# The first 512 up columns begun on two tiles of 128 tokens, the third tile following, with the next columns and the conv weights moved forward

## The chip, the cores and the metric

The kernel runs on one core of one Trainium2 chip. What counts is the device time of one execution, in microseconds (us), read as the median of several runs. The engines are PE (TensorE: matmuls, and transposes as matmuls with an identity), DVE (VectorE), ACT (ScalarE), POOL (GpSimd) and SP (SyncE, which issues almost all weight loads as DMAs). Each engine works off its own instructions in a fixed order; an instruction that has to wait holds up everything behind it on the same engine. SBUF is the on-chip memory that the engines read, PSUM the small memory (8 banks) that PE writes its products to.

## The reference

One layer of a flow-matching trunk on 384 tokens (128 context tokens, 256 latent tokens) with 2048 channels, in float32:

```python
def _layer(x, mod, grid, s_ret0, c0, n0, m0, lp):
    ...
    sh1, sc1, g1, sh2, sc2, g2 = jnp.split(mod, 6, axis=-1)
    h = _ln(x) * (1.0 + sc1) + sh1
    mix, states = _mixer(h, ...)                       # w_in, heads, out = (...) @ w_out
    x = _ln(ALPHA * x + g1 * mix) * ln1_g + ln1_b
    h = _ln(x) * (1.0 + sc2) + sh2
    x = _ln(ALPHA * x + g2 * _ffn(h, ...)) * ln2_g + ln2_b

def _ffn(h, grid, w_up, conv_ff, w_down):
    ug = h @ w_up                                      # 2048 x 2*5504
    u, g = ug[..., :D_FF], ug[..., D_FF:]
    return (jax.nn.silu(_seq_conv(u, conv_ff, grid)) * g) @ w_down
```

The vectors `sh1 ... g2` come from `mod = silu(c) @ w_mod + b_mod`, one set for the context tokens and one for the latent ones. The convolution has 3 taps along the tokens.

## The kernel before, in words

**Precision.** Each float32 operand is split in a high part (`hi`, `ah`: a cast, on ACT) and a rest (`lo`, `al`: source minus high part, on DVE or POOL; the helper's line is L118), and each product is three matmuls: high by high, and the two mixed ones.

**Tiles.** The 384 tokens are three tiles of 128. In the projections up and in, a weight block 128x128 is PE's stationary operand and all 384 tokens move past it, so the product comes out transposed, with channels on the partitions (`psu`, L182 to L184, 128x384). The projections out (`w_out`) and down keep a tile of tokens stationary and move 512 weight columns (L190 to L192).

**Weights.** One load is 512 KB, 128x1024 elements (for the up projection 4 blocks of 128 rows by 256 columns, a "group" here). It goes into one of 4 `raw` buffers, is cast into one of 3 `hi` buffers and subtracted into one of 3 `lo` buffers. SP issues the loads in order; a load waits until its `raw` buffer is free.

**Around the change.** The last 512 columns of `w_out` are done tile by tile with all weights already split (five groups in buffers of their own, `wxh` and `wxl`, three in `hi` and `lo`). After each tile comes its norm chain, `norms(tt)`: DVE scales the product by the gate, adds it to the residual `r` and takes statistics; POOL raises the variance to the power -1/2 (`brs`, L200), DVE applies the first norm in two passes over 128x2048 (L981, L983), takes statistics again (`xst`, L1063), adds epsilon (`veps`, L198), POOL's power comes again, DVE makes the scaled mean `nm` (L963) and ACT writes the normalised tile in four pieces (L1069: into `g1b` for tile 0, `xn` for tile 1, `l1g` for tile 2). `h2_piece` then takes 128 channels of a tile: PE transposes them into a bank of the 3-bank pool `pat` (`xtp`, L114), ACT (or DVE) applies scale and shift (`h`, 5 buffers), ACT casts `ah`, POOL (or DVE) makes `al`.

The first 512 up columns (256 of u, 256 of g) need all three tiles, since all 384 tokens move in one matmul; the pieces of tiles 1 and 2 are made together then (128x256, on DVE). Their products lie in the 5-bank pool `pmm`. `up_gate` applies convolution, silu and gate to u and g (DVE: L345, L349, L1159, and the split of the result, `fal`). The other up columns follow, 256 of u and 256 of g at a time; "the second 512 columns" below are the next ones.

**The vector sums.** Besides, the vector g2 of `mod` (`mods5`) is summed on DVE: 32 loads `mraw` of 512 KB by SP (3 buffers), and for each two passes of 128x1024 (`macc`: L283 for the first load, L286 after). They are not needed before the final residual, but stand in DVE's and SP's order from the first up columns on.

**Order.** The program states dependences and a written order; a scheduler that estimates times fixes the order on each engine when the program is built. `issue_after` holds an instruction's place in that order behind another's. So the order is not that of the source, and a changed source moves instructions elsewhere too.

**The names the change touches.** `norms` and `h2_piece` (above), `ps_first` (the banks of the first 512 columns), `up_product` and `up_gate`, `mod_from_rows` (scale and shift vectors read back from memory: `mfr`, then a transpose `mfp`), and `cfr`, `pcf`, `cfw` (conv weights: load, transposes, copy).

Of the kernel before, what the change touches and what calls it, by code (L numbers as in the profile page):

```python
# [21 lines left out]
NT = T // P  # L22
# [60 lines left out]
def hybrid_step(ctx, tc, ca, cb, x_prompt, x_sample, state_ret, state_c, state_n, state_m, c, c_ctx,  # L83
# [3 lines left out]
    nc = tc.nc  # L87
# [5 lines left out]
    wraw = pool("wraw", 4)  # L93
# [12 lines left out]
    ident = cst[:, C_ID:C_ID + P]  # L106
# [4 lines left out]
        return prompt[0] if tt == 0 else sample[0, (tt - 1) * P:tt * P, :]  # L111

    def transpose(out, in_, n=P):
        nc.tensor.transpose(out, in_, ident[:n, :n])  # L114

    def split(dst_hi, dst_lo, src, eng=None):
        nc.scalar.copy(dst_hi, src)  # L117
# [17 lines left out]
    def rows_bcast(dst, src_row, n):  # L135
        nc.gpsimd.dma_start(out=dst, in_=src_row.to_broadcast([P, n]))
# [34 lines left out]
    act_hi = [None] * KT  # L171
    act_lo = [None] * KT
# [6 lines left out]
    def mm_a(ps, w, kk, width, m, ah, al, start, stop):  # L179
        hi, lo = w  # L180
        s = slice(kk * width + m * P, kk * width + (m + 1) * P)
        nc.tensor.matmul(ps, lhsT=hi[:, s], rhs=ah, start=start, stop=False)  # L182
        nc.tensor.matmul(ps, lhsT=hi[:, s], rhs=al, start=False, stop=False)  # L183
        nc.tensor.matmul(ps, lhsT=lo[:, s], rhs=ah, start=False, stop=stop)  # L184

    def mm_b(ps, w, kk, ah, al, tt, start, stop, c0=0, n=512):
        hi, lo = w
        s = slice(kk * 512 + c0, kk * 512 + c0 + n)
        t = slice(tt * P, (tt + 1) * P)
        nc.tensor.matmul(ps, lhsT=ah[:, t], rhs=hi[:, s], start=start, stop=False)  # L190
        nc.tensor.matmul(ps, lhsT=ah[:, t], rhs=lo[:, s], start=False, stop=False)  # L191
        nc.tensor.matmul(ps, lhsT=al[:, t], rhs=hi[:, s], start=False, stop=stop)  # L192
# [2 lines left out]

    def rstd(out, var, n=1):
        v = small.tile([P, NT], F32, tag="veps", name="veps")
        nc.vector.tensor_scalar(out=v[:, :n], in0=var, scalar1=EPS, scalar2=None, op0=ALU.add)  # L198
        with tc.high_priority():
            mark["pow"] = nc.gpsimd.tensor_tensor(out=out, in0=v[:, :n], in1=mhalf[:, :n], op=ALU.pow).ins  # L200

# [119 lines left out]
            yield from g  # L321

    def mod_from_rows(part, n, psp, sbp, name, plus):
        rows = sbp.tile([2 * KT, P], F32, tag="mfr", name="mfr", bufs=1)
        for v in range(2):
            nc.sync.dma_start(out=rows[v * n:(v + 1) * n, :], in_=modrow[part, v, :n * P].rearrange("(k p) -> k p", p=P))
        ps = psp.tile([P, 2, n], F32, tag="ps", name="mfp")
        transpose(ps.rearrange("p v k -> p (v k)"), rows[:2 * n, :], 2 * n)
        nc.vector.tensor_scalar(out=modf[name][:, :, :n], in0=ps, scalar1=plus, scalar2=None, op0=ALU.add)
# [613 lines left out]

    rp = pool("rp", 1, reuse_waits="tile")
    r = [rp.tile([P, D], F32, name=f"r{tt}") for tt in range(NT)]

    rstat = [rp.tile([P, 5, 6], F32, name=f"rst{tt}") for tt in range(NT)]

# [37 lines left out]
    with ExitStack() as p2:  # L986
# [23 lines left out]
        def w_out_block(nb):  # L1010
            ps = pso if nb == 0 else [(pat if nb == 1 else pmm).tile([P, 512], F32, tag="ps", name="pso")
                                      for _ in range(NT)]
            for k0 in (12,) if nb == 0 else range(0, KT, 2):
                part_b(ps, weights_b(wo, k0, 2, (nb * 512,)), 2, k0, 0, KT - 1 if nb else 13)
                if nb > 0:
                    mods4.step()
                if k0 == (10 if nb else 12):
                    residual_loads(nb)
                if nb == 2 and k0 == 14:
                    residual_loads(3)  # L1020
                if nb == 1 and k0 == 8:
# [17 lines left out]
        for i in range(KT // 2):  # L1039
            raw = wraw.tile([P, 1024], F32, tag="raw", name="raw")  # L1040
            nc.sync.dma_start(out=raw.rearrange("p (k n) -> p k n", k=2),
                              in_=wo[2 * i * P:(2 * i + 2) * P, 1536:2048].rearrange("(k p) n -> p k n", p=P))
            if i < KT // 2 - 3:
                hi = wx.tile([P, 1024], F32R, name=f"wxh{i}")
                lo = wx.tile([P, 1024], F32R, name=f"wxl{i}")
                split(hi, lo, raw)
                ws.append((hi, lo))
            else:
                ws.append(split_weights(raw))
        xn = [None] * NT  # L1050

        def norms(tt):
            residual(sb2, g1b, tt, 3, ps[tt], True, True)
            if tt == NT - 1:
                mark["pb1"] = mark["pow"]
            st = post_stats(tt)
            if tt == NT - 1:
                mark["pa2"] = mark["pow"]
            for s in post_norm(tt, st, l1g, l1b, 1):
                pass  # L1060
            xst = small.tile([P, 4, 6], F32, tag="bst", name="xst")
            for j in range(4):
                nc.vector.bn_stats(out=xst[:, j, :], in_=r[tt][:, j * 512:(j + 1) * 512])  # L1063
            mv, rs = aggr(xst)
            nm = neg_scaled_mean(mv, rs)
            t = l1g if tt == NT - 1 else g1b[:, 0, :] if tt == 0 else xnp.tile([P, D], F32, tag="xn", name="xn")
            for j in range(4):
                s = slice(j * 512, (j + 1) * 512)
                nc.scalar.activation(t[:, s], r[tt][:, s], AF.Identity, bias=nm, scale=rs)  # L1069
            xn[tt] = t  # L1070
# [20 lines left out]

        for tt in range(NT):
            for kt in range(KT):
                mm_b(ps[tt], ws[kt // 2], kt % 2, act_hi[kt], act_lo[kt], tt, kt == 0, kt == KT - 1)
                if tt == NT - 1 and kt >= 5:
                    h2_piece(0, kt - 5)
            norms(tt)
        for kt in range(KT - 5, KT):
            h2_piece(0, kt)
        for kt in range(5):  # L1100
            h2_piece(1, kt)
        wu, wd = w_up[0], w_down[0]
        ps_first = [pmm.tile([P, T], F32, tag="ps", name="psu") for _ in range(2)]
        wg = None
        for i in range(KT + 2):
            if i < 5:
                h2_piece(2, i)
            elif i < KT:
                h2_piece(1, i, 2)
            if i == KT - 1:  # L1110
                mark["h2"] = mark["lo"]
            kt = i - 2
            if kt < 0:
                continue
            if kt % 4 == 0:
                if kt < 12:
                    with tc.issue_after(mark["pb1"] if kt < 4 else mark["pa2"]):
                        wg = weights_a(wu, kt, 4, 0, 256)
                else:
                    wg = weights_a(wu, kt, 4, 0, 256)  # L1120
            for m in range(2):
                mm_a(ps_first[m], wg, kt % 4, 256, m, new_hi[kt], new_lo[kt], kt == 0, kt == KT - 1)
        act_hi[:], act_lo[:] = new_hi, new_lo


# [3 lines left out]
    ffp = pool("ffp", 12, p3, reuse_waits="tile")  # L1129
    sb3 = pool("sb3", 2, p3, reuse_waits="tile")  # L1130
    acc = [g2p.tile([P, D], F32, name=f"acc{tt}") for tt in range(NT)]
    cfr = sb3.tile([NF, 3, P], F32, tag="y", name="cfr")
    nc.gpsimd.dma_start(out=cfr, in_=conv_ff[0].rearrange("t (f p) -> f t p", p=P))
    cfw = g2p.tile([P, 3, NF], F32, name="cfw")
    pcf = pat.tile([P, 3, NF], F32, tag="ps", name="pcf")
    for t in range(3):
        transpose(pcf[:, t, :], cfr[:, t, :], NF)
    nc.vector.tensor_copy(cfw, pcf)
    def up_product(pool_, ug, f0, n):
        cols = n * P  # L1140
        ps = [pool_.tile([P, T], F32, tag="ps", name="psu") for _ in range(n)]
# [21 lines left out]
            out.append((ah, al))  # L1163
        return out

    a = up_gate(0, ps_first, up_product(pmm, 1, 0, 2))
    psum_a.close()
    pps = pool("pps", 8, p3, space=PSUM, reuse_waits="tile")

    def ups(f0, n):  # L1170
        out = []
        for f in range(f0, f0 + n, 2):
            m = min(2, f0 + n - f)
            us = up_product(pps, 0, f, m)
            out += up_gate(f, us, up_product(pps, 1, f, m))
        return out

# [43 lines left out]
    ws = []  # L1221
# [64 lines left out]
```

## Time and profile before

| what | value |
|---|---|
| median of 3 runs | 2062.88 us (2061.55 to 2065.3) |
| profiled execution | 2066.21 us, of it span 2064.4 us |
| mean granted TensorE clock | 0.982 |
| PE busy | 1988.4 us (96%) |
| DVE busy | 1231.4 us (60%) |
| ACT busy | 694.1 us (34%) |
| POOL busy | 233.0 us (11%) |
| last matmuls of w_out begin | 921.44 us |
| first up matmul | 941.33 us |
| first 512 up columns end | 979.07 us |
| second 512 up columns end | 1017.3 us |

Positions in the table are microseconds from the start of the profiled span. In rows of a timeline the first number is the start, the second the length, then engine, line, operation, out<-in, shape and count; square brackets give the idle time before it and what ended it. In the view of stretches each engine has its busy time and its count; the last three columns are the granted TensorE clock (1.00 is full), the DMA engines' busy share and GB/s. Matmuls overlap, so the time that one costs is the distance between starts, not its length.

### The profile page before, as it was taken

To read this page: it belongs to the slowest core of one execution; us is meant where nothing else is said; L and a number is where in the kernel's file an instruction comes from. 1 tells how busy PE (TensorE), PEld (TensorE's weight loads), DVE (VectorE), ACT (ScalarE), POOL (GpSimd) and SP (SyncE) were. 2 spreads that over 40 slices of the span, in tenths; PEclk is the share of its full clock that TensorE was granted. 3 is DMA by queue.
4 is the path that set the end of the run, shared out by engine and by line. 5 is a ranking of instruction groups with operands and counts; after the bars stand their busy time and mean duration, and the time that the engine had idled before them with its cause. 6 is when DMAs were issued, how large, how long until landed. Compare 5 with 4: busy or idle time off the path is not lost.

```text
span 2064.4 us, 26334 instructions
## 1 busy us (share of the span) xinstructions
PE 1988.4 (96%) x10233; PEld 1752.6 (85%) x10233; DVE 1231.4 (60%) x1791; ACT 694.1 (34%) x1052; POOL 233.0 (11%) x226
## 2 busy tenths in 40 slices
PE   6899998999999998998999999999999999999995
PEld 4677888898888876678999889999889998999984
DVE  3655795487978894577944323477334444444478
ACT  3223324333343443235233333333222332333331
POOL 0001332221222231021000000000000000000004
PEclk9999999999999999998999999999999999999998
DMA  9895679587769765834744334465334444434342
GB/s 342 246 309 183 179 194 160 118 219 209 249 193 198 186 199 185 306 108 138 245 123 123 127 128 123 123 206 178 127 128 123 123 142 145 128 106 143 113 153 102
DMA packets 260637, 352.30 MB, mean 171 GB/s; under 512 B 16143, under 2 KB 200784, under 8 KB 259360
## 3 DMA queue, kind: packets, MB, share of 16 engines
q1 hardware_dynamic: 256240, 340.08, 55.4%
q0 software_dynamic: 4272, 10.54, 1.5%
q8 instruction: 80, 1.31, 0.3%
q14 instruction: 45, 0.37, 0.1%
HBM read 343.16 MB, written 7.41 MB: 170 GB/s over the span
## 4 chain that ended last, share of the span: by engine, by line
PE 82%; DVE 8%; DMA 3%; issue 3%; POOL 1%; SPq 1%; ACT 1%; POOLq 0%; DVEq 0%; ACTq 0%
PE psu L184 12%; PE psu L182 12%; PE psu L183 12%; PE psd L192 5%; PE psd L191 5%; PE psd L190 5%; PE psa L182 4%; PE psa L184 4%; PE psa L183 4%; PE psb L190 3%; PE psb L191 3%; PE psb L192 3%; DVE macc L286 3%; DMA mraw<-in_w_mod 2%; PE modps L255 2%
## 5 line engine op out<-in xcount | busy, mean ns | idle before, releaser
L118 DVE TENSOR_TENSOR lo<-raw,hi 128x1024 fp32r<-128x1024 f32 (+4 forms) x443 | 481.6, 1094 | 561.3 <-ACT hi L117 560.6
L117 ACT CAST hi<-raw 128x1024 fp32r<-128x1024 f32 (+4 forms) x473 | 434.9, 929 | 971.4 <-PE psu L183 353.2
L183 PE MATMUL psu<-al,hi 128*128 128x384 f32 x1376 | 467.6, 340 | 0.0
L184 PE MATMUL psu<-ah,lo 128*128 128x384 f32 x1376 | 464.5, 340 | 2.5 <-DVE lo L118 2.5
L182 PE MATMUL psu<-ah,hi 128*128 128x384 f32 x1376 | 466.4, 340 | 0.0
L286 DVE SCALAR_TENSOR_TENSOR macc<-mraw,ct,macc 128x1024 f32<-128x1024 f32 x210 | 286.9, 1392 | 16.2 <-DMA mraw<-in_w_mod 16.2
L184 PEld LDWEIGHTS psu<-ah,lo 128*128 128x128 f32 x1376 | 259.0, 188 | 2.9 <-DVE lo L118 2.9
L182 PEld LDWEIGHTS psu<-ah,hi 128*128 128x128 f32 x1376 | 259.1, 189 | 1.8 <-issue 0.8
L183 PEld LDWEIGHTS psu<-al,hi 128*128 128x128 f32 x1376 | 259.3, 188 | 0.2
L192 PE MATMUL psd<-hi,fal 128*128 128x512 f32 (+1 forms) x484 | 192.1, 397 | 0.0
L191 PE MATMUL psd<-lo,fah 128*128 128x512 f32 (+1 forms) x484 | 189.9, 392 | 0.0
L190 PE MATMUL psd<-hi,fah 128*128 128x512 f32 (+1 forms) x484 | 186.7, 390 | 0.0
L184 PE MATMUL psa<-ah,lo 128*128 128x384 f32 x512 | 176.1, 346 | 7.5 <-DVE lo L118 7.5
L182 PE MATMUL psa<-ah,hi 128*128 128x384 f32 x512 | 180.5, 357 | 1.7 <-ACT hi L117 1.7
L183 PE MATMUL psa<-al,hi 128*128 128x384 f32 x512 | 175.8, 344 | 0.0
L191 PE MATMUL psb<-lo,ah 128*128 128x512 f32 x384 | 154.5, 402 | 0.6 <-DVE lo L118 0.6
L192 PE MATMUL psb<-hi,al 128*128 128x512 f32 x384 | 153.3, 399 | 0.0
L190 PE MATMUL psb<-hi,ah 128*128 128x512 f32 x384 | 149.8, 405 | 0.0
L182 PEld LDWEIGHTS psa<-ah,hi 128*128 128x128 f32 x512 | 97.4, 191 | 17.7 <-issue 11.6
L191 PEld LDWEIGHTS psd<-lo,fah 128*128 128x128 f32 x484 | 90.9, 188 | 23.1
L190 PEld LDWEIGHTS psd<-hi,fah 128*128 128x128 f32 x484 | 90.9, 188 | 21.1
L192 PEld LDWEIGHTS psd<-hi,fal 128*128 128x128 f32 x484 | 90.9, 188 | 20.7
(301 smaller groups left out, 2244.0 us busy)
## 6 DMA issues: line engine op xcount, KB each, us to landing
raw<-in_w_up SPq DMA_DIRECT2D x168, 512.0 KB, 3.8
mraw<-in_w_mod SPq DMA_DIRECT2D x112, 512.0 KB, 4.9
raw<-in_w_down SPq DMA_DIRECT2D x84, 512.0 KB, 3.6
raw<-in_w_in SPq DMA_DIRECT2D x128, 256.0 KB, 4.9
raw<-in_w_in SPq DMA_DIRECT2D x52, 512.0 KB, 7.2
wm<-in_w_mod SPq DMA_DIRECT2D x20, 1024.0 KB, 8.8
raw<-in_w_out SPq DMA_DIRECT2D x32, 512.0 KB, 5.1
wm<-in_w_mod SPq DMA_DIRECT2D x16, 768.0 KB, 6.9
```

The lines of the kernel that those rows point to most:

```text
L117: nc.scalar.copy(dst_hi, src)
L118: mark["lo"] = (eng or nc.vector).tensor_tensor(out=dst_lo, in0=src, in1=dst_hi.bitcast(F32), op=ALU.subtract).ins
L182: nc.tensor.matmul(ps, lhsT=hi[:, s], rhs=ah, start=start, stop=False)
L183: nc.tensor.matmul(ps, lhsT=hi[:, s], rhs=al, start=False, stop=False)
L184: nc.tensor.matmul(ps, lhsT=lo[:, s], rhs=ah, start=False, stop=stop)
L190: nc.tensor.matmul(ps, lhsT=ah[:, t], rhs=hi[:, s], start=start, stop=False)
L191: nc.tensor.matmul(ps, lhsT=ah[:, t], rhs=lo[:, s], start=False, stop=False)
L192: nc.tensor.matmul(ps, lhsT=al[:, t], rhs=hi[:, s], start=False, stop=stop)
L255: nc.tensor.matmul(ps[32 * g:32 * g + 32, :w], lhsT=ct[:, kt, :], rhs=raw[:, kk * w:(kk + 1) * w], start=kt < 4, stop=kt >= 12)
L286: nc.vector.scalar_tensor_tensor(out=acc[:, v, :], in0=raw, scalar=ct[:, kt, v:v + 1], in1=acc[:, v, :], op0=ALU.mult, op1=ALU.add)
```

## The change

- **First 512 columns in two steps.** Tiles 0 and 1 go first: 192 matmuls with 256 tokens moving (instead of 384), into four banks `early`. Tile 2 follows with the operands exchanged: the tile is stationary and 256 weight columns move (`late`, 96 matmuls, one bank of `pat`, L1141). ACT copies the two halves of `late` out, and four transposes put them into the third part of the `early` banks.
- **All 8 groups of these columns stay split** until tile 2 has used them: five in the buffers of the w_out weights (now `wuh`, `wul`), three in `hi` and `lo`. Their splits are placed after `mark["tile1"]`, the epsilon of tile 1's second norm.
- **Pieces one by one.** Tile 1's pieces are made like tile 0's (ACT, ACT, POOL), tile 2's on DVE and ACT.
- **Next u columns early.** `second`, the u half of the second 512 columns, is issued into free banks of `pat` before `up_gate(0)`.
- **Conv weights early**, in the third block of w_out; `mfr` shares two buffers with other row tiles (tag `rt`) instead of having its own; the matmuls of the last w_out block are placed behind the last transpose.

```diff
     def mod_from_rows(part, n, psp, sbp, name, plus):
-        rows = sbp.tile([2 * KT, P], F32, tag="mfr", name="mfr", bufs=1)
+        rows = sbp.tile([2 * KT, P], F32, tag="rt", name="mfr")
...
+                    cfr = sb2.tile([NF, 3, P], F32, tag="rt", name="cfr")
+                    nc.gpsimd.dma_start(out=cfr, in_=conv_ff[0].rearrange("t (f p) -> f t p", p=P))
+                if nb == 2 and k0 == 14:
+                    pcf = pat.tile([P, 3, NF], F32, tag="ps", name="pcf")
...
         for tt in range(NT):
             for kt in range(KT):
-                mm_b(ps[tt], ws[kt // 2], kt % 2, act_hi[kt], act_lo[kt], tt, kt == 0, kt == KT - 1)
+                with tc.issue_after(mark["pe"]):
+                    mm_b(ps[tt], ws[kt // 2], kt % 2, act_hi[kt], act_lo[kt], tt, kt == 0, kt == KT - 1)
...
             norms(tt)
+            if tt == 1:
+                mark["tile1"] = mark["veps"]
...
-        ps_first = [pmm.tile([P, T], F32, tag="ps", name="psu") for _ in range(2)]
...
+        early = [[pmm.tile([P, T], F32, tag="ps", name="psu") for _ in range(2)] for _ in range(2)]
+        ws_up = {}
+        for kt in range(KT):
+            if kt % 4 == 0:
+                for ug in range(2):
+                    raw = wraw.tile([P, 1024], F32, tag="raw", name="raw")
...
+                    i = kt // 2 + ug
+                    with tc.issue_after(mark["tile1"]):
+                        if i < 5:
+                            hi = wx.tile([P, 1024], F32R, name=f"wuh{i}", tag=f"wxh{i}")
+                            lo = wx.tile([P, 1024], F32R, name=f"wul{i}", tag=f"wxl{i}")
+                            split(hi, lo, raw)
+                            ws_up[kt // 4, ug] = hi, lo
+                        else:
+                            ws_up[kt // 4, ug] = split_weights(raw)
             h2_piece(1, kt)
+            if kt >= 8:
+                h2_piece(2, 2 * kt - 16)
+                h2_piece(2, 2 * kt - 15)
+            for ug in range(2):
+                for m in range(2):
+                    mm_a(early[ug][m][:, :2 * P], ws_up[kt // 4, ug], kt % 4, 256, m,
+                         new_hi[kt][:, :2 * P], new_lo[kt][:, :2 * P], kt == 0, kt == KT - 1)
+        late = pat.tile([P, 2, 256], F32, tag="ps", name="psl")
+        ts = slice(2 * P, T)
+        for ug in (1, 0):
+            for n, kt in enumerate([kt for kg in (3, 2, 1, 0) for kt in range(4 * kg, 4 * kg + 4)]):
+                hi, lo = ws_up[kt // 4, ug]
+                cols = slice(kt % 4 * 256, kt % 4 * 256 + 256)
+                for a, b in ((new_hi, hi), (new_hi, lo), (new_lo, hi)):
+                    nc.tensor.matmul(late[:, ug, :], lhsT=a[kt][:, ts], rhs=b[:, cols],
+                                     start=n == 0 and b is hi and a is new_hi, stop=n == KT - 1 and a is new_lo)
+        rows = sb2.tile([P, 512], F32, tag="rt", name="late")
+        for ug in (1, 0):
+            nc.scalar.copy(rows[:, ug * 256:ug * 256 + 256], late[:, ug, :])
+        for ug in (1, 0):
             for m in range(2):
-                mm_a(ps_first[m], wg, kt % 4, 256, m, new_hi[kt], new_lo[kt], kt == 0, kt == KT - 1)
+                c0 = ug * 256 + m * P
+                transpose(early[ug][m][:, ts], rows[:, c0:c0 + P])
...
-    a = up_gate(0, ps_first, up_product(pmm, 1, 0, 2))
+    second = up_product(pat, 0, 2, 2)
+    a = up_gate(0, *early)
...
-            us = up_product(pps, 0, f, m)
+            us = second if f == 2 else up_product(pps, 0, f, m)
```

Three places of the built order, of before and of the change.

**DVE, tile 1's second norm** (`r_6868` is tile 1's residual, `r_6869` tile 2's; `pso` is the w_out product). Before:

```order
L1063 BN_STATS xst<-r_6868 128x6 x4
L118 TENSOR_TENSOR lo<-raw,hi 128x1024
L210 BN_AGGR bmv<-xst 128x2
L118 TENSOR_TENSOR lo<-raw,hi 128x1024
L952 TENSOR_TENSOR rtmp<-pso,g1b 128x512
L198 TENSOR_SCALAR veps<-bmv 128x1
L118 TENSOR_TENSOR lo<-raw,hi 128x1024
L954 SCALAR_TENSOR_TENSOR r_6869<-r_6869,rtmp 128x512
L963 SCALAR_TENSOR_TENSOR nm<-bmv,brs 128x1
```

Three splits stand among the statistics and tile 2's residual. The same place in the changed kernel:

```order
L1067 BN_STATS xst<-r_6868 128x6 x4
L210 BN_AGGR bmv<-xst 128x2
L198 TENSOR_SCALAR veps<-bmv 128x1
L118 TENSOR_TENSOR wul_7883<-raw,wuh_7882 128x1024
L118 TENSOR_TENSOR wul_7889<-raw,wuh_7888 128x1024
L118 TENSOR_TENSOR wul_7967<-raw,wuh_7966 128x1024
L118 TENSOR_TENSOR wul_7973<-raw,wuh_7972 128x1024
L964 SCALAR_TENSOR_TENSOR nm<-bmv,brs 128x1
L953 TENSOR_TENSOR rtmp<-pso,g1b 128x512
L955 SCALAR_TENSOR_TENSOR r_6869<-r_6869,rtmp 128x512
```

The statistics up to epsilon now stand together, four weight splits stand between epsilon and `nm`, and tile 2's residual stands behind `nm`.

**SP, the loads of the up weights and of the vector sums.** Before:

```order
L1041 DMA raw<-in_w_out 128x2x512 x8
L141 DMA raw<-in_w_up 128x4x256 x9
L234 DMA mraw<-in_w_mod 128x1024 x3
L141 DMA raw<-in_w_up 128x4x256
L234 DMA mraw<-in_w_mod 128x1024 x2
```

The nine loads of up weights at its start are all that stands between the last w_out load and the first `mraw`. Changed:

```order
L1114 DMA raw<-in_w_up 128x4x256 x8
L141 DMA raw<-in_w_up 128x4x256 x7
L234 DMA mraw<-in_w_mod 128x1024 x5
L141 DMA raw<-in_w_up 128x4x256
L234 DMA mraw<-in_w_mod 128x1024
```

Now fifteen loads stand ahead of the first `mraw`: the eight of the first 512 columns and seven more.

**DVE, from the splits of the second 512 columns to the split of their last group of g** (the `lo` of the last row). Before, the last rows of this piece:

```order
L1159 TENSOR_TENSOR y<-y,psu 128x384
L118 TENSOR_TENSOR lo<-raw,hi 128x1024
L286 SCALAR_TENSOR_TENSOR macc<-mraw,ct,macc 128x1024
L1159 TENSOR_TENSOR y<-y,psu 128x384
L286 SCALAR_TENSOR_TENSOR macc<-mraw,ct,macc 128x1024
L118 TENSOR_TENSOR fal<-y,fah 128x384
L286 SCALAR_TENSOR_TENSOR macc<-mraw,ct,macc 128x1024
L118 TENSOR_TENSOR fal<-y,fah 128x384
L286 SCALAR_TENSOR_TENSOR macc<-mraw,ct,macc 128x1024 x5
L118 TENSOR_TENSOR lo<-raw,hi 128x1024
```

Five passes stand in a row ahead of that split. Changed, the last rows of the same piece:

```order
L286 SCALAR_TENSOR_TENSOR macc<-mraw,ct,macc 128x1024
L345 SCALAR_TENSOR_TENSOR y<-psu,cfw,y 128x127
L349 SCALAR_TENSOR_TENSOR y<-psu,cfw,y 128x4x63
L286 SCALAR_TENSOR_TENSOR macc<-mraw,ct,macc 128x1024
L345 SCALAR_TENSOR_TENSOR y<-psu,cfw,y 128x127
L349 SCALAR_TENSOR_TENSOR y<-psu,cfw,y 128x4x63
L286 SCALAR_TENSOR_TENSOR macc<-mraw,ct,macc 128x1024 x7
L118 TENSOR_TENSOR lo<-raw,hi 128x1024
```

Seven stand there now, and taps of the convolution of the next u columns between the passes ahead of them. In the whole piece, from the first L283 row to this last `lo`, the changed order has on DVE: L283 twice, 20 passes L286, 5 splits of 128x1024, 8 pairs L345 and L349, and 4 operations of 128x384 (two L1179, two `fal`). Before the first L283 row stand three of the four splits of `second`, directly behind each other.

More of the change, by code (lines that the diff above doesn't have):

```diff
@@ L113, in transpose @@
     def transpose(out, in_, n=P):
-        nc.tensor.transpose(out, in_, ident[:n, :n])
+        mark["pe"] = nc.tensor.transpose(out, in_, ident[:n, :n]).ins
     def split(dst_hi, dst_lo, src, eng=None):
@@ L197, in rstd @@
         v = small.tile([P, NT], F32, tag="veps", name="veps")
-        nc.vector.tensor_scalar(out=v[:, :n], in0=var, scalar1=EPS, scalar2=None, op0=ALU.add)
+        mark["veps"] = nc.vector.tensor_scalar(out=v[:, :n], in0=var, scalar1=EPS, scalar2=None, op0=ALU.add).ins
         with tc.high_priority():
@@ L945, in hybrid_step @@
     r = [rp.tile([P, D], F32, name=f"r{tt}") for tt in range(NT)]
+    cfw = rp.tile([P, 3, NF], F32, name="cfw")
     rstat = [rp.tile([P, 5, 6], F32, name=f"rst{tt}") for tt in range(NT)]
@@ L1025, in w_out_block @@
                     rows_bcast(l1b, ln1_b, D)
+                    cfr = sb2.tile([NF, 3, P], F32, tag="rt", name="cfr")
+                    nc.gpsimd.dma_start(out=cfr, in_=conv_ff[0].rearrange("t (f p) -> f t p", p=P))
+                if nb == 2 and k0 == 14:
+                    pcf = pat.tile([P, 3, NF], F32, tag="ps", name="pcf")
+                    for t in range(3):
+                        transpose(pcf[:, t, :], cfr[:, t, :], NF)
+                    nc.vector.tensor_copy(cfw, pcf)
                 if nb == 2 and k0 == 8:
@@ L1043, in hybrid_step @@
             if i < KT // 2 - 3:
-                hi = wx.tile([P, 1024], F32R, name=f"wxh{i}")
-                lo = wx.tile([P, 1024], F32R, name=f"wxl{i}")
+                hi = wx.tile([P, 1024], F32R, name=f"wxh{i}", tag=f"wxh{i}")
+                lo = wx.tile([P, 1024], F32R, name=f"wxl{i}", tag=f"wxl{i}")
                 split(hi, lo, raw)
@@ L1053, in norms @@
             residual(sb2, g1b, tt, 3, ps[tt], True, True)
-            if tt == NT - 1:
-                mark["pb1"] = mark["pow"]
             st = post_stats(tt)
-            if tt == NT - 1:
-                mark["pa2"] = mark["pow"]
             for s in post_norm(tt, st, l1g, l1b, 1):
@@ L1097, in hybrid_step @@
             norms(tt)
+            if tt == 1:
+                mark["tile1"] = mark["veps"]
         for kt in range(KT - 5, KT):
             h2_piece(0, kt)
-        for kt in range(5):
-            h2_piece(1, kt)
-        wu, wd = w_up[0], w_down[0]
-        ps_first = [pmm.tile([P, T], F32, tag="ps", name="psu") for _ in range(2)]
[L1104 to L1120, printed above, removed]
+        wu, wd = w_up[0], w_down[0]
@@ new lines, in hybrid_step @@
+        early = [[pmm.tile([P, T], F32, tag="ps", name="psu") for _ in range(2)] for _ in range(2)]
[4 more added lines that the diff above has]
+                    raw = wraw.tile([P, 1024], F32, tag="raw", name="raw")
+                    nc.sync.dma_start(out=raw.rearrange("p (k n) -> p k n", k=4),
+                                      in_=wu[kt * P:(kt + 4) * P, ug * DFF:ug * DFF + 256]
+                                      .rearrange("(k p) n -> p k n", p=P))
+                    i = kt // 2 + ug
[7 more added lines that the diff above has]
+                            ws_up[kt // 4, ug] = split_weights(raw)
+            h2_piece(1, kt)
+            if kt >= 8:
[5 more added lines that the diff above has]
+                         new_hi[kt][:, :2 * P], new_lo[kt][:, :2 * P], kt == 0, kt == KT - 1)
@@ L1131, in hybrid_step @@
     acc = [g2p.tile([P, D], F32, name=f"acc{tt}") for tt in range(NT)]
[L1132 to L1138, printed above, removed]
     def up_product(pool_, ug, f0, n):
```

## The prediction

> **What bounds the kernel now.** First the page: the busy times, then the chain of work that ended last.
>
> ```profile
> PE 1988.4 (96%) x10233; PEld 1752.6 (85%) x10233; DVE 1231.4 (60%) x1791; ACT 694.1 (34%) x1052; POOL 233.0 (11%) x226
> PE 82%; DVE 8%; DMA 3%; issue 3%; POOL 1%; SPq 1%; ACT 1%; POOLq 0%; DVEq 0%; ACTq 0%
> ```
>
> PE is the bound on average, but an average says nothing about the stage that is changed. So next the view of stretches, cut where the stages change (length, then PE, PEld, DVE, ACT, POOL busy, clock, DMA share, GB/s).
>
> ```profile
> 930.00:941.30 11.30, 5.83 (x18) 3.11 (x19) 8.23 (x17) 9.96 (x32) 9.02 (x17) 0.50 0.06 23
> 960.00:979.00 19.00, 19.00 (x110) 18.70 (x109) 18.26 (x26) 8.43 (x11) 0.00 (x0) 1.00 0.79 255
> 979.00:992.30 13.30, 13.30 (x76) 12.98 (x74) 13.30 (x14) 4.95 (x7) 0.00 (x0) 1.00 0.72 230
> 994.80:999.30 4.50, 4.46 (x17) 4.46 (x17) 4.50 (x4) 0.00 (x0) 0.00 (x0) 0.62 0.81 258
> ```
>
> Up to 941.3 PE is half idle at half clock, behind ACT and POOL (the norm chain). From then on PE is full, and DVE is full as well: 18.26 of 19.0 and 13.3 of 13.3 us. Here DVE has no slack, and the work it does in between is mostly the vector sums. Whether that has already cost PE something is told by the waits of PE, and by its own rows:
>
> ```profile
> PE psu L184 <- DVE lo L118: 2.5, 1, 2.5
> ...
> 941.33 0.99 PE L182 MATMUL psu<-ah,hi 128*128 128x384 f32 x2
> 978.89 0.34 PE L184 MATMUL psu<-ah,lo 128*128 128x384 f32 x1
> 987.38 0.34 PE L184 MATMUL psu<-ah,lo 128*128 128x384 f32 x1
> 991.62 0.34 PE L184 MATMUL psu<-ah,lo 128*128 128x384 f32 x1
> 994.84 0.44 PE L184 MATMUL psu<-ah,lo 128*128 128x384 f32 x1 [2.54 <-DVE lo L118]
> 1000.18 0.34 PE L184 MATMUL psu<-ah,lo 128*128 128x384 f32 x1
> ```
>
> The first up matmul starts at 941.33; the 192nd at 978.89, so the first 512 columns end near 979.07. The rows at 987.38 and 991.62 are 24 matmuls apart: 4.24/24 = 0.1767 us each. The row at 1000.18 is 24 after 991.62 but 8.56 us later: 4.32 lost, 2.54 of it the wait for a split on DVE and 1.78 the low clock after it (0.62 in the stretch above). So DVE's queue already reaches PE once before the change. That is the place to watch.
>
> **Part 1, from the norm to the first up matmul.** The changed order puts tile 1's statistics ahead of the splits, but four splits ahead of its `nm`; on POOL 14 `al` of tile 0 stand ahead of the power that `nm` needs (5 more than before), and on ACT two weight casts, three `h`, one more cast and three `ah` stand between `xn` and the first up matmul.
>
> ```profile
> L118 POOL TENSOR_TENSOR al<-h,ah x21: 443/452/2497, 918.4 to 938.0; 128x128 fp32r<-128x128 f32 x21
> L200 POOL TENSOR_TENSOR brs<-veps,mhalf x12: 544/962/2607, 10.9 to 2049.8; 128x1 f32<-128x1 f32 x12
> 927.66 2.50 POOL L118 TENSOR_TENSOR al<-h,ah 128x128 fp32r<-128x128 f32 x1
> 927.48 2.36 DVE L981 SCALAR_TENSOR_TENSOR r<-r,bmv,l1g 128x2048 f32<-128x2048 f32 x1
> 927.39 2.92 ACT L1069 ACTIVATE xn<-r,nm,brs 128x512 f32<-128x512 f32 x4
> L117 ACT CAST hi<-raw 128x1024 fp32r<-128x1024 f32 x6 | 6.3, 1050 | 4.9 <-PE psu L183 3.7 <-PE pso L192 1.1
> 916.97 1.16 ACT L1084 ACTIVATE h<-xtp,sh,sc 128x128 f32<-128x128 f32 x3 [2.92 <-PE xtp L114]
> 918.01 0.70 ACT L117 CAST ah<-h 128x128 fp32r<-128x128 f32 x3
> ```
>
> An `al` alone takes 0.45 us on POOL, but 2.50 when it meets DVE's 2.36 us pass: POOL stands while such a DVE operation runs. Over the whole stage 21 of them took 918.4 to 938.0, 0.93 us each. The first price goes by that pace: 14 x 0.93 = 13.0 from 918.4, so 931.4; the power 0.96; `xn` at 932.4 to 935.3 (before 927.39 to 930.3); then 3 casts x 1.05 + 1.16 + 0.70 = 5.0: first up matmul at 940.3. The other end is POOL never held: then ACT is the limit: 14 pieces x (1.16 + 0.70)/3 = 8.7 and two casts 2.1 from 916.97, so 927.7; the power 0.96, `nm` and `xn` to 931.9, and 5.0 after it: 936.9. Both ends are estimates from these rows. I take 939.0, nearer the first, because the four splits are DVE operations of the kind that held POOL.
>
> The Trainium skill (page "SBUF — State Buffer", section "SBUF: two separate sides") says that a DVE operation with two SBUF inputs and a GpSimd operation that reads SBUF exclude each other for the whole instruction, and whichever starts first has the ports. The 2.50 us row agrees. By that rule each of the four splits lets one `al` through, and the rest, behind the splits, go at 0.45: first up matmul near 937.5, and the time 1.5 us below my forecast, still in its range.
>
> **Part 2, the first 512 columns.** What a 256-wide matmul and a transpose cost is read from two places (the down projection's end has 256-wide matmuls):
>
> ```profile
> 2039.43 0.28 PE L190 MATMUL psd<-hi,fah 128*128 128x256 f32 x1
> 2042.18 0.28 PE L192 MATMUL psd<-hi,fal 128*128 128x256 f32 x1
> 945.37 0.27 PE L114 MATMUL xtp<-cst,xn 128*128 128x128 f32 x1
> 945.48 0.27 PE L114 MATMUL xtp<-cst,l1g 128*128 128x128 f32 x1
> 962.41 0.38 PE L114 MATMUL pcf<-cst,cfr 43*128 43x43 f32 x3
> ```
>
> 23 steps in 2.75 us: 0.1196 each; a transpose 0.11. Removed: 192 x 0.1767 = 33.9, 16 transposes 1.8, the three of `pcf` 0.35; that is 36.0 of the 37.74 us, and the remaining 1.7 is the half clock after the idle time. Added: (192 + 96) x 0.1196 = 34.4, 26 transposes 2.9; with 1.7 to 2.7 of half clock (PE starts on a trickle of pieces; I take 2.2) 39.5. The exchange of operands itself is thus no gain: 288 steps of 256 for 192 of 384 are the same columns. First 512 columns end (E, when `second` begins) at 939.0 + 39.5 = 978.5, and `pcf`, now in w_out, pushes all of it by 0.35: 978.85 against 979.07, a gain of 0.2. With the ends of part 1 and of the half clock, 976 to 981. ACT's two copies of `late` lie beside PE's work on `second`; the four transposes behind them add 0.44.
>
> **Part 3, the second 512 columns.** Here the moved loads count. The order has three splits of `second` on DVE ahead of the first vector sum, and seven loads of SP ahead of the first `mraw`. The seventh needs the `raw` buffer of the third split; that split's `hi` buffer holds the last u group of the first columns, which `late` reads in its 49th to 60th matmul of 96, so till E - 36 x 0.1196 = E - 4.3. ACT's cast 1.05, the split 1.2: E - 2.0; then SP's loads and the landing of `mraw`:
>
> ```profile
> 954.59 0.50 SPq L234 DMA_DIRECT2D mraw<-in_w_mod  x1
> DMA to landing us min/median/max: 3.2/3.5/5.0
> 962.78 1.41 DVE L283 TENSOR_SCALAR macc<-mraw,ct 128x1024 f32<-128x1024 f32 x2
> 970.23 0.34 DVE L345 SCALAR_TENSOR_TENSOR y<-psu,cfw,y 128x127 f32<-128x127 f32 x1
> 970.87 1.21 DVE L118 TENSOR_TENSOR lo<-raw,hi 128x1024 fp32r<-128x1024 f32 x1
> 981.46 1.22 DVE L118 TENSOR_TENSOR lo<-raw,hi 128x1024 fp32r<-128x1024 f32 x1
> 982.60 1.28 DVE L286 SCALAR_TENSOR_TENSOR macc<-mraw,ct,macc 128x1024 f32<-128x1024 f32 x1
> 983.79 0.55 DVE L1159 TENSOR_TENSOR y<-y,psu 128x384 f32<-128x384 f32 x1
> 984.26 1.28 DVE L286 SCALAR_TENSOR_TENSOR macc<-mraw,ct,macc 128x1024 f32<-128x1024 f32 x1
> 987.59 6.06 DVE L286 SCALAR_TENSOR_TENSOR macc<-mraw,ct,macc 128x1024 f32<-128x1024 f32 x5
> 993.57 1.22 DVE L118 TENSOR_TENSOR lo<-raw,hi 128x1024 fp32r<-128x1024 f32 x1
> ```
>
> SP's issue and a landing of 3.5 to 5.0 (the loads are dense here) put the first sum at E + 3.3; before it was at 962.78, 16.3 ahead of E. Up to the split of g's last group DVE must work off, start to start: the first two passes 1.33, 20 passes x 1.195 (five took 5.98), 5 splits x 1.14 (981.46 to 982.60), 8 pairs of taps x 0.64 (970.23 to 970.87), 4 small ones x 0.47 (983.79 to 984.26): 1.3 + 23.9 + 5.7 + 5.1 + 1.9 = 37.9. The same sum over the rows of before gives 30.8, and 962.78 + 30.8 = 993.6 is where its split stands, so DVE runs without a gap in such a piece. The split ends at E + 41.3. PE needs it after `second` (96 matmuls, 17.0), three groups of g (72, 12.7) and the 0.44: E + 30.1. PE waits 11.2 and then loses about 1.8 to the clock, as it did before; before's 4.32 goes. Net 11.2 + 1.8 + 0.44 - 4.32 = +9.1. DVE catches up behind it: the splits after that come before PE asks for them (the next, near E + 46, is needed near E + 47), so nothing is added later, and nothing is given back, since PE is full for the rest. What is queued behind the passes is exactly those splits; the vector sums have no reader until the end.
>
> **Sum.** -0.2 + 9.1 = +8.9 on 2066.21 (the profiled execution): 2075.1. That execution lies 3.3 above the median, so on the median 2062.88 + 8.9 = **2071.8**. With part 1's ends and the landing's, 2068 to 2075.
>
> **Rivals.**
> - **The gate on SP is not where I put it**: the loads of `mraw` go out before the third split. Then the first sum starts right behind the three splits, at E - 2, 5.3 earlier; the wait is 5.9, the sum +3.6: 2066.5. For it: SP's `raw` buffers may come free by another path. Against: three splits stand ahead of the sums on DVE in any case.
> - **No wait at all, the other side**: the sums do not reach the split, because `mraw` comes late enough or early enough that DVE has the split done by E + 30. It decides at a first sum before E - 8. Then 4.32 is gone and 0.44 added: -0.2 - 3.9 = -4.1: 2058.8, and 2056 if POOL is not held in part 1. For it: before, the first sum was at E - 16. Against: the buffer that `late` holds until E - 4.3.
> - **`mfr` is late.** It now waits for a buffer that PE reads until about 879.3, and takes long to land:
>
> ```profile
> 878.38 0.95 PE L264 MATMUL modf<-cst,mr 128*128 128x2 f32 x8
> DMA to landing us min/median/max: 8.2/8.4/8.6
> ```
>
>   Its transpose stands where PE comes by at about 885.6 (estimated from the order). A landing of 8.4 after 879.3 and SP's issue is 888.7 at worst: 3.1 of wait and 1.8 of clock on top: 2076.7. Against: these landings were measured among other loads; at a shorter one it costs nothing.
>
> **How the numbers follow.** My forecast 0.64; gate elsewhere 0.13; no wait 0.11; `mfr` late 0.12. A measurement of this kernel can tell about 0.2%, 4.1 us, from no change: 2058.8 to 2067.0. No wait lies at the faster edge: 0.09 faster, 0.02 same. The gate's case is same (0.11) or slightly slower (0.02). So faster 0.09, same 0.13, slower 0.78. The range for 8 in 10 leaves out "no wait" and the far ends of the others: 2064 to 2078.
>
> **What would show it.** Right: in the waits of PE, `psu L184 <- DVE lo L118` once with 9 to 13 us, in the second 512 columns; the first L283 row some 3 us behind the first matmul of `second`, and DVE without a gap from there to the split; a first up matmul at 937 to 941; the clock near 0.6 after the wait. Wrong: no such wait; first sums ahead of E; a first up matmul before 936 or after 942; a wait of PE on `mfp`'s load near 886; or PE waiting in the first 512 columns for pieces (ACT, POOL) by more than 2 us, which I have at nothing beyond the clock.

## The result, and the profile after

The changed kernel takes 2072.94 us (median of 5 runs, 2071.38 to 2076.54), the kernel before 2061.55 in the runs beside it (2058.37 to 2065.3): a ratio of 1.0058, 95% interval 1.0042 to 1.0074. So it is slower by about 11 us (9 to 15 by the interval). The forecast was 2071.8, the range 2064 to 2078.

The page of the changed kernel, its busy times:

```profile
PE 1980.8 (96%) x10333; PEld 1747.5 (84%) x10333; DVE 1231.3 (59%) x1791; ACT 700.2 (34%) x1076; POOL 244.6 (12%) x237
```

PE is busy 7.6 us less than before and the kernel is longer: PE waits more. Where it waits is told by the waits of PE (engine and instruction, what it waited for, total, times, longest), in the part of the program around the change:

```profile
PE psu L182 <- DVE y L349: 13.7, 1, 13.7
PE xtp L114 <- ACT h L1088: 7.6, 6, 3.9
PE xtp L114 <- ACT xn L1073: 3.2, 1, 3.2
```

The two waits for ACT in the norm chain are there as before (7.4 and 2.9). New is one wait of 13.7 us, in place of the 2.5 us for a split. Its surroundings in the stretches (length, then PE, PEld, DVE, ACT, POOL, clock, DMA share, GB/s):

```profile
938.30:973.10 34.80, 34.47 (x293) 34.11 (x293) 16.08 (x39) 15.60 (x41) 6.09 (x13) 1.00 0.17 51
973.10:991.20 18.10, 18.07 (x105) 17.72 (x103) 13.21 (x18) 7.62 (x11) 0.00 (x0) 1.00 0.71 238
991.20:1004.80 13.60, 0.00 (x0) 0.00 (x0) 13.60 (x20) 2.59 (x6) 0.00 (x0) 0.69 0.71 231
1004.80:1010.00 5.20, 5.16 (x16) 5.19 (x17) 5.20 (x6) 1.04 (x2) 0.00 (x0) 0.50 0.53 164
```

In the third row PE does nothing and DVE does not stop: DVE's queue sets the end here. Its rows in that stretch, with PE's around them:

```profile
973.08 0.34 PE L182 MATMUL psu<-ah,hi 128*128 128x384 f32 x1
990.83 0.33 PE L184 MATMUL psu<-ah,lo 128*128 128x384 f32 x1
1004.84 0.66 PE L182 MATMUL psu<-ah,hi 128*128 128x384 f32 x1 [13.67 <-DVE y L349]
1010.40 0.34 PE L182 MATMUL psu<-ah,hi 128*128 128x384 f32 x1
...
977.99 1.42 DVE L283 TENSOR_SCALAR macc<-mraw,ct 128x1024 f32<-128x1024 f32 x2 [6.64 <-PE psu L184]
1003.95 0.35 DVE L345 SCALAR_TENSOR_TENSOR y<-psu,cfw,y 128x127 f32<-128x127 f32 x1
1004.21 0.48 DVE L349 SCALAR_TENSOR_TENSOR y<-psu,cfw,y 128x252 f32<-128x252 f32 x1
1006.44 8.46 DVE L286 SCALAR_TENSOR_TENSOR macc<-mraw,ct,macc 128x1024 f32<-128x1024 f32 x7
1014.80 1.23 DVE L118 TENSOR_TENSOR lo<-raw,hi 128x1024 fp32r<-128x1024 f32 x1
```

`second` begins at 973.08 (E of the prediction) and the first vector sum runs at 977.99. The forecast had PE stop at the split of g's last group (the row at 1014.80). PE stops earlier, three matmuls into g: its next matmul writes the second g product, and in the built program that one lies in the PSUM bank that holds the first of the two products of `second`, called the early u products below. The bank is free when the last taps have read that product, and these taps (L345, L349 at 1003.95 to 1004.69) stand in DVE's queue behind the same vector sums. From 1004.84 the low clock costs another 2.4 us: 18 matmuls in 5.56 us, where 0.1767 each would be 3.18.

**How the two executions add up.** Executions differ ahead of the change: tile 0's normalised tile begins at 911.12 in the profiled execution of before and at 905.95 in that of the change. From that point to the end of the span the change takes 1164.05 us against 1153.28: 10.8 more. By stages, on before's time axis (5.17 added): the first 512 columns end at 978.25 instead of 979.07 (-0.8), the four late transposes +0.44, the wait +13.67, the low clock +2.4, and before's 4.32 are gone: +11.4. The 0.6 between the two sums is not assigned to a stage.

### The profile page after: what moved, and what is told of

The parts are those of the page before. It is cut to its first block, busy times and chain, and to the rows that moved or that the text cites. A ratio compares the mean times of both kernels' runs of the same rounds, so it can differ in the third digit from the quotient of the medians.

```text
span 2070.0 us, 26571 instructions
## 1 busy us (share of the span) xinstructions
PE 1980.8 (96%) x10333; PEld 1747.5 (84%) x10333; DVE 1231.3 (59%) x1791; ACT 700.2 (34%) x1076; POOL 244.6 (12%) x237
## 4 chain that ended last, share of the span: by engine, by line
PE 82%; DVE 8%; DMA 3%; issue 3%; POOL 1%; SPq 1%; ACT 1%; POOLq 0%; DVEq 0%; ACTq 0%
PE psu L183 11%; PE psu L182 11%; PE psu L184 11%; PE psd L192 5%; PE psd L190 5%; PE psd L191 5%; PE psa L182 4%; PE psa L184 4%; PE psa L183 4%; PE psb L190 3%; PE psb L191 3%; PE psb L192 3%; DVE macc L286 3%; DMA mraw<-in_w_mod 2%; PE modps L255 2%
## 5 line engine op out<-in xcount | busy, mean ns | idle before, releaser
L118 DVE TENSOR_TENSOR lo<-raw,hi 128x1024 fp32r<-128x1024 f32 (+4 forms) x438 | 475.9, 1094 | 558.3 <-ACT hi L117 557.6
L117 ACT CAST hi<-raw 128x1024 fp32r<-128x1024 f32 (+4 forms) x468 | 429.7, 928 | 967.4 <-PE psu L183 364.0
L182 PE MATMUL psu<-ah,hi 128*128 128x384 f32 (+1 forms) x1336 | 450.2, 339 | 13.7 <-DVE y L349 13.7
L183 PE MATMUL psu<-al,hi 128*128 128x384 f32 (+1 forms) x1336 | 451.5, 338 | 0.0
L184 PE MATMUL psu<-ah,lo 128*128 128x384 f32 (+1 forms) x1336 | 449.4, 338 | 0.0
L286 DVE SCALAR_TENSOR_TENSOR macc<-mraw,ct,macc 128x1024 f32<-128x1024 f32 x210 | 287.8, 1397 | 16.0 <-DMA mraw<-in_w_mod 15.9
L182 PEld LDWEIGHTS psu<-ah,hi 128*128 128x128 f32 x1336 | 250.5, 188 | 15.8 <-issue 14.8
L183 PEld LDWEIGHTS psu<-al,hi 128*128 128x128 f32 x1336 | 251.6, 188 | 0.1
L184 PEld LDWEIGHTS psu<-ah,lo 128*128 128x128 f32 x1336 | 251.3, 188 | 0.0
L184 PE MATMUL psa<-ah,lo 128*128 128x384 f32 x512 | 175.0, 343 | 7.5 <-DVE lo L118 7.2
L182 PE MATMUL psa<-ah,hi 128*128 128x384 f32 x512 | 179.1, 355 | 1.7 <-ACT hi L117 1.7
L182 PEld LDWEIGHTS psa<-ah,hi 128*128 128x128 f32 x512 | 96.4, 189 | 17.7 <-issue 11.6
```

What stands on the lines that cost most here:

```text
L118: mark["lo"] = (eng or nc.vector).tensor_tensor(out=dst_lo, in0=src, in1=dst_hi.bitcast(F32), op=ALU.subtract).ins
L286: nc.vector.scalar_tensor_tensor(out=acc[:, v, :], in0=raw, scalar=ct[:, kt, v:v + 1], in1=acc[:, v, :], op0=ALU.mult, op1=ALU.add)
```

## The experiments

The kernel before ran beside each group; its medians differ a little between groups (2061.6 to 2063.1 us), so each result stands with its own ratio. Run again beside the last group, the change was where it had been:

> The changed kernel itself, beside these runs of the kernel before, as the measure for the experiments: 2072 to 2074 us, ratio 1.005 to 1.006.

Measured: 2072.71 us, ratio 1.0051 (1.0037 to 1.0065). Ratios within 0.0015 of each other say nothing. A finer measure, though of one execution per kernel, is the time from ACT's first write of tile 0's normalised tile to the end of the span: 1164.05 us in the first profiled execution of the change and 1164.08 in this one (907.32 to 2071.4). It is used in experiments 4, 6, 7 and 9.

**1. Free banks.** The g half of the second 512 columns goes to two banks that nobody holds at that time.

```diff
...
     a = up_gate(0, *early)
+    second_g = up_product((pmm, pat), 1, 2, 2)
     psum_a.close()
...
-            out += up_gate(f, us, up_product(pps, 1, f, m))
+            out += up_gate(f, us, second_g if f == 2 else up_product(pps, 1, f, m))
```

> The changed kernel, with the g half of the second 512 columns put into two banks of PSUM that are free (the fifth of the up pool and the one of the late product) instead of the next two of the new pool, one of which still holds the product of the early u columns. Theory A, the bank decides: the wait of 13.7 us and the 2.4 us of low clock after it go, since the built order now also has only 10 instead of 20 passes of the vector sums ahead of the split of g's last group: 2072.9 - 16 = 2057 us. Theory B, the queue on DVE decides and the bank is only where PE meets it first: PE waits at the split of g's last group instead, some 10 us, 2069 to 2072 us.

Measured: 2065.45 us, ratio 1.0015 (1.0006 to 1.0023): between the two theories. The wait at the bank is gone, but the waits of PE show another one, in the third 512 columns:

```profile
PE psu L184 <- DVE lo L118: 5.4, 1, 5.4
...
1025.72 0.69 PE L184 MATMUL psu<-ah,lo 128*128 128x384 f32 x1 [5.36 <-DVE lo L118]
```

Five passes stand directly ahead of that split on DVE. With the banks free the built order had put the split of g's last group ahead of half the passes, so this run changed two things: the bank and the order. Neither theory is decided by it.

**2. Held sums.** Each pass of the vector sums must follow, in DVE's order, the weight split that stands before it in the written order.

```diff
             if f0 >= 4:
-                mods5.step()
+                with tc.issue_after(mark["lo"]):
+                    mods5.step()
```

> The changed kernel, with each pass of the vector sums held behind the last weight split that stands before it in the written order, so that none runs in the second 512 columns; banks as in the change. Theory B, the queue on DVE decides: the taps that free the bank run about 3 us after the early u columns are done, so a wait of some 3 us and 1 us of low clock stays: 2060 us. Theory A in its pure form, the bank is lost whatever DVE does: the wait stays above 8 us, 2067 us or more.

Measured: 2059.36 us, ratio 0.9986 (0.9977 to 0.9995). The bank is the same as in the change, and the wait at it:

```profile
995.27 0.42 PE L182 MATMUL psu<-ah,hi 128*128 128x384 f32 x1 [1.13 <-DVE y L349]
```

1.13 us instead of 13.67. The bank is lost for long only because the taps stand behind the sums: theory A in its pure form is out.

**3. The kernel before with held sums.** The same edit on the kernel before.

> The kernel before, with the same hold on the vector sums. If the 4.32 us that I read at its split (2.54 of wait, 1.78 of low clock) were the price of the vector sums ahead of it, they go: 4 us less than before, 2057 us. If another split or load takes their place: no difference.

Measured: 2057.64 us, ratio 0.998 (0.9971 to 0.9989), 4.4 us less than the kernel before beside it (2062.03). Among the waits of PE in this part none for a split is left:

```profile
PE xtp L114 <- ACT h L1084: 7.2, 8, 2.9
PE xtp L114 <- ACT l1g L1069: 2.9, 1, 2.9
```

So the 4.32 us read at before's split (2.54 of wait, 1.78 of clock) fit as the price of the sums there.

**4. Free banks and held sums.** Both edits on the change.

> The changed kernel with free banks and held sums. Both theories: no wait in the second 512 columns, 2056 us. What is left against the kernel before with held sums is the gain of the first 512 columns alone, which my sum has at 0.2 us and which the trace has at 0.8 us less 0.4 for the four transposes: 0 to 1 us.

Measured: 2056.74 us, ratio 0.9978 (0.9969 to 0.9987). No wait of PE is left in the second 512 columns. Against the kernel before with held sums (2057.64) that is 0.9 us less, which the two intervals don't tell from nothing. From tile 0's normalised tile on the two take the same: 1147.73 us here, 1147.64 there. So without the sums in the way, no gain of the changed matmuls is shown.

**5. Free banks, the same queue.** Free banks again, but DVE's order of the change is kept: the split of g's last group is held behind 22 passes (for which the vector sums are set up earlier in the source). Up to that split DVE has the same operations as in the change, some taps a pass earlier or later, so that there in the main only the bank differs.

```diff
...
+            if f0 == 2 and ug and k0 == 12:
+                for _ in range(11):
+                    next(mods5.gen)
+                with tc.issue_after(mark["macc"]):
+                    w = weights_a(wu, k0, 4, ug * DFF + f0 * P, cols)
...
```

> Free banks as in the first experiment, but DVE's order of the change kept: the split of g's last group in the second 512 columns is held behind 22 passes of the vector sums. Step of the prediction (the split ends 37.9 us after the first sum, PE needs it 30 us after the start of the early u columns): with the first sum at 978 in the trace of the change the split ends near 1016, PE needs it near 1003.5, so a wait of 12 to 13 us at L184 and no wait at the bank; 2070 to 2073 us, as the change itself. If the bank alone is the cause: no wait of that size, 2057 to 2065 us.

Measured: 2072.83 us, ratio 1.0045 (1.0033 to 1.0058): the time of the change, without its bank. First sum, last passes and splits on DVE, and PE's wait:

```profile
980.78 1.42 DVE L283 TENSOR_SCALAR macc<-mraw,ct 128x1024 f32<-128x1024 f32 x2 [7.01 <-DMA mraw<-in_w_mod]
1010.42 7.26 DVE L286 SCALAR_TENSOR_TENSOR macc<-mraw,ct,macc 128x1024 f32<-128x1024 f32 x6
1017.60 3.50 DVE L118 TENSOR_TENSOR lo<-raw,hi 128x1024 fp32r<-128x1024 f32 x3
...
1018.88 1.01 PE L184 MATMUL psu<-ah,lo 128*128 128x384 f32 x2 [12.39 <-DVE lo L118]
```

This is the step of the prediction itself: 36.8 us from the first sum to the start of the split, and PE stands 12.4 us at L184. Nothing but DVE's queue held that split: its operand `hi` was cast by ACT at 1005.64 to 1006.69. The bank in the change only stops PE earlier in the same stretch; the wait at the split, which would have come next, is then covered by it. What decides is DVE's queue.

**6. The late product frees its buffers sooner.** Group by group instead of all of g first; nothing else in DVE's order moves.

```diff
-        for ug in (1, 0):
-            for n, kt in enumerate([kt for kg in (3, 2, 1, 0) for kt in range(4 * kg, 4 * kg + 4)]):
+        for kg in (3, 2, 1, 0):
+            for ug, kt in [(ug, kt) for ug in (1, 0) for kt in range(4 * kg, 4 * kg + 4)]:
...
```

> The changed kernel, with the late product read group by group from the last (u and g of each group together) instead of all g first, so that the hi buffer for which the third split waits is free 36 matmuls (4.3 us) sooner. Nothing else in DVE's order changes. If the gate on SP (third split, seventh load, then the sums' loads) sets the first sum: its load is issued 4.3 us earlier, the first sum is at most 4.3 us earlier, the taps' own inputs take back about 1 us of it: 2069 to 2070 us. If the landing or something else sets it: 2073 us.

Measured: 2072.23 us, ratio 1.0045 (1.0032 to 1.0059): no difference that the ratios show; from tile 0's normalised tile on it is 1162.40 us, 1.65 less than the change. The trace shows why it is so little. In the change, ACT's cast for the third split, SP's rows and the landing of the sums' loads (of the six up to 986.7; the first took 6.1) are:

```profile
969.04 1.05 ACT L117 CAST hi<-raw 128x1024 fp32r<-128x1024 f32 x1 [3.18 <-PE psl L1141]
965.73 6.01 SPq L141 DMA_DIRECT2D raw<-in_w_up  x3
971.80 10.36 SPq L234 DMA_DIRECT2D mraw<-in_w_mod  x5
DMA to landing us min/median/max: 3.2/6.1/7.6
```

and in this run (of the six up to 988.3; the first took 8.1):

```profile
968.66 1.05 ACT L117 CAST hi<-raw 128x1024 fp32r<-128x1024 f32 x1 [0.35 <-PE psl L1141]
968.18 3.19 SPq L141 DMA_DIRECT2D raw<-in_w_up  x3
971.42 2.03 SPq L234 DMA_DIRECT2D mraw<-in_w_mod  x3
DMA to landing us min/median/max: 3.2/8.1/9.3
...
979.63 1.42 DVE L283 TENSOR_SCALAR macc<-mraw,ct 128x1024 f32<-128x1024 f32 x2 [8.66 <-DMA mraw<-in_w_mod]
```

This execution runs 2.16 us later than that of the change (first up matmul at 934.65 against 932.49), so the load went out 2.5 us sooner (969.26 against 971.80 on the change's time axis), not 4.3, and landed 2 us slower; the first sum came 0.5 us sooner. The 4.3 of the expectation was miscounted: the third `hi` buffer is free after 36 matmuls of `late` instead of 60, so 24 matmuls or 2.8 us sooner. The gate, the third split, is still the gate and moved by those 2.5 us. But now the three weight loads ahead of it go out within 3.2 us instead of 6.0, and the sums' load lands later behind them. So the gate was not the only thing that held the first sum.

**7. More buffers for the scaled pieces.**

```diff
-            h = sb2.tile([P, 2 * P], F32, tag="h2", name="h2", bufs=5)[:, :w]
+            h = sb2.tile([P, P], F32, tag="h2", name="h2", bufs=10)
```

> The changed kernel with 10 buffers of 128x128 instead of 5 of 128x256 for the scaled pieces, so that ACT does not wait for POOL. In the trace of the change ACT waits 2.65 us for POOL's al in three places ahead of tile 1's normalisation. If POOL, held by DVE's splits, sets the start of the up projection through these buffers: the first up matmul comes some 2.6 us earlier and the time falls by 2 us, to 2071. If al is needed at the same time anyway, or the norm chain on DVE sets it: no difference, 2073.

Measured: 2071.31 us, ratio 1.0036 (1.0023 to 1.0049). From ACT's first write of tile 0's normalised tile to the first up matmul it is 23.85 us (908.71 to 932.56) against 26.54 in the change (905.95 to 932.49) and 30.21 before (911.12 to 941.33). In the waits of ACT in that stretch of the change there is

```profile
ACT h L1088 <- POOL al L118: 3.1, 4, 1.2
```

and in this run no such row. So POOL's pace did set the start of the up projection through the five buffers, by 2.7 us, as expected. In the time, the ratio lies 0.0015 to 0.0022 (3 to 4.5 us) below the change's two, about its uncertainty; from tile 0's normalised tile on the run takes 1159.19 us, 4.9 less than the change. Not all of that is the buffers' doing. In the built program of this run `late` and not `second` lies in the bank of the second g product, so the wait at the bank is gone here too, with the change's order of DVE. What PE waits for instead:

```profile
1007.95 0.69 PE L182 MATMUL psu<-ah,hi 128*128 128x384 f32 x1 [4.85 <-ACT hi L117]
1015.90 0.69 PE L184 MATMUL psu<-ah,lo 128*128 128x384 f32 x1 [6.95 <-DVE lo L118]
```

The first is a cast that stands on ACT behind the activation of the early u product, and that waits for the taps on DVE; the second is the split of g's last group behind its seven passes. Together 11.8 us: without having been built for it, this run repeats the fifth.

**8. The early issue of the next u columns undone**, with held sums.

```diff
-    second = up_product(pat, 0, 2, 2)
...
-            us = second if f == 2 else up_product(pps, 0, f, m)
+            us = up_product(pps, 0, f, m)
```

> Held sums as in the second experiment, and the early issue of the next u columns undone: they use the new pool's first bank, which holds one of the first u products until its taps are done. If issuing them early into free banks is worth something: PE waits behind the late product for ACT's copies, the transposes, ACT's scaling and four pairs of taps, about 5 us, and 1.7 us of low clock, in place of the 1.1 us at the bank in the second experiment: 2059.4 + 5 = 2064 to 2065 us. If it hides nothing: 2059 us.

Measured: 2063.89 us, ratio 1.0011 (1.0002 to 1.002), 4.5 us above the second experiment (0.0025 by the ratios). PE's rows behind the late product:

```profile
974.78 0.28 PE L1141 MATMUL psl<-wuh,al 128*128 128x256 f32 x1
975.52 0.71 PE L114 MATMUL psu<-cst,late 128*128 128x128 f32 x4 [0.46 <-ACT late L1145]
979.59 0.66 PE L182 MATMUL psu<-ah,hi 128*128 128x384 f32 x1 [3.36 <-DVE y L349]
```

Without `second` there is a gap of 0.46 and 3.36 us behind the late product, and the low clock after it. `second` hides it; that part of the change does what it is for.

**9. Everything together**: free banks, held sums, the late product group by group, ten buffers.

> Free banks, held sums, late product group by group, ten h buffers, all on the changed kernel. The free banks with held sums gave 2056.7. The late order should add nothing once the sums are held (no wait is left there); the buffers up to 2 us if they do so alone: 2054.5 to 2057.

Measured: 2057.43 us, ratio 0.9971 (0.996 to 0.9983), the lowest ratio of all, though not distinguishable from the fourth experiment (0.9978) or from the kernel before with held sums (0.998); from tile 0's normalised tile on it is 1148.21 us, not less than the fourth's 1147.73. PE's wait in the first 512 columns changes its form:

```profile
PE psu L183 <- POOL al L118: 2.2, 1, 2.2
```

The first up matmul comes 2.9 us earlier against ACT's first write of tile 0 than in the change (907.4 to 931.05, so 23.65, against 26.54), but PE then stands 2.2 us for POOL's `al`: at the first matmul with `al` (934.51, and 934.02 in the change) only 1.0 us is left (27.1 against 28.1).

## Why the prediction was right, and where not

- **Direction and cause**: right. It was DVE's queue: the vector sums start 21 us later against the first 512 columns, and PE, which needs DVE's work at a fixed place behind them, waits. Experiments 2 and 5 show it from both sides: without the sums the wait is 1.1 us; with the sums and without the bank it is 12.4.
- **The size of the change**: +8.9 was forecast, 11.4 measured. That the time forecast lies only 1.1 us off is luck in part: it stood on 2062.88 for the kernel before, which took 2061.55 in the runs beside the change.
- **The place of the wait**: wrong. The prediction has PE wait at the split of g's last group, L184. It waits at the first matmul into a bank, L182. The step that failed is in part 3, "PE needs it after `second` (96 matmuls, 17.0), three groups of g": it counted PE's way through g as free. Which bank g would get was not looked at. The rival that should have stood there: a PSUM bank that the early u product keeps until its taps are done.
- **The size of the wait**: 11.2 was forecast, 13.67 measured at the bank, 12.39 at the split (experiment 5). The term of DVE's work was right (37.9 against 38.0, from 977.99 to the end of the split at 1016.03). Mis-sized was the first sum, E + 3.3 against E + 4.9 (E + 5.3 in experiment 5): the landing of `mraw` took 6.1 us, outside the 3.2 to 5.0 of before. What slowed it is not separated by a run. Before, it took 5.0, with a weight load 0.4 us ahead of it and the next two sums' loads 5.0 and 5.4 behind; in the change a weight load goes out 0.4 ahead and two sums' loads only 0.6 and 1.0 behind. In experiment 6, with the other two weight loads closer ahead as well, it took 8.1. In experiment 5 PE got 0.9 us further than forecast, four matmuls into g's last group.
- **The clock after the wait**: 1.8 forecast, 2.4 measured.
- **The rival "gate elsewhere"** did not come: the third split ends at 971.35, the seventh weight load goes out at 971.38 and the first sum's load at 971.80, E - 1.3, as the prediction's gate has it (E - 2.0). But moving the gate by 2.5 us moves the first sum by 0.5 us only (experiment 6).
- **The rival "`mfr` is late"** did not come: no wait of PE on its data is in the trace.
- **Part 2**: 978.25 for the end of the first 512 columns on before's time axis, forecast 978.85. Up to there the stage took 40.6 us from its first matmul, forecast 39.5; PE ran at 0.50 from 932.4 to 938.3.
- **Part 1**: the number was near (937.66 on before's time axis, forecast 939.0), but a step of it was wrong, so that the nearness is luck. The prediction's estimate by the rule of the Trainium skill, page "SBUF — State Buffer", section "SBUF: two separate sides", was 937.5; it counted the same `al`. I had 14 `al` ahead of the power that `nm` needs. In the trace, POOL, DVE and ACT of the change:

```profile
915.98 1.48 POOL L200 TENSOR_TENSOR brs<-veps,mhalf 128x1 f32<-128x1 f32 x1
917.44 6.78 POOL L118 TENSOR_TENSOR al<-h,ah 128x128 fp32r<-128x128 f32 x9
...
915.83 5.15 DVE L118 TENSOR_TENSOR wul<-raw,wuh 128x1024 fp32r<-128x1024 f32 x4
920.90 0.40 DVE L964 SCALAR_TENSOR_TENSOR nm<-bmv,brs 128x1 f32<-128x1 f32 x1
...
925.06 2.92 ACT L1073 ACTIVATE xn<-r,nm,brs 128x512 f32<-128x512 f32 x4
```

  The power runs at 915.98, behind 4 `al` only (14 stand ahead of the next one, at 927.09, which belongs to tile 2's first norm); `nm` then waits behind DVE's four splits until 920.90, and `xn` begins at 925.06 because ACT first works off tile 0's pieces, at POOL's pace. POOL is slow there: 9 `al` in 6.78 us, 0.75 each, where one alone takes 0.45. Taken singly, the three that run beside DVE's splits take 1.06, 1.43 and 1.43 us, the one that meets DVE's residual (L955, two inputs in SBUF) 0.90, and the other five 0.45 or 0.46, also where DVE reads `pso` from PSUM (L953). That DVE's splits are what slows POOL agrees with that rule of the Trainium skill; no run here took the splits away. That POOL's pace set ACT's is shown (experiment 7).

## What to carry to other kernels

When a change moves loads or buffers, ask what on a second, full engine starts later because of it: here work that nobody needs soon kept its place in front of work that PE needs next, and holding it back (experiments 2 to 4) was worth more than the change to the matmuls. Follow a product to the bank it is written to, not only to its operands. And an earlier issue of a load is not an earlier landing when other loads are issued earlier with it.

## What the runs showed of the hardware that was not expected

- The first load of the vector sums, 512 KB, landed 5.0 us after its issue before, 6.1 in the change and 8.1 in experiment 6. From issue to landing the DMA engines were 0.62, 0.85 and 0.97 busy, at 210, 283 and 300 GB/s: the more other loads were on their way, the later it landed.
- The low clock after a wait of PE costs about the same after a short and a long one: 1.78 us after 2.54, 2.4 after 3.36 (experiment 8: 16 matmuls in 5.25 us, where 0.1767 each would be 2.83), 2.4 after 13.67. After the 1.13 of experiment 2 no low clock is seen: from the second matmul on they are 0.18 apart. After the 12.39 of experiment 5 the matmuls are 0.32 apart, not 0.18, until 4.0 us after PE's restart.
